# Issue order in the pooling stage of a two-layer decoder trunk: sums, transposes and the next layer's units

## The chip, the cores and the metric

The kernel runs on one core of a Trainium2 chip. The metric is the device time of one execution in microseconds (us), as the median of several runs; a profiled execution of the kernel before stands beside it. TensorE is called PE here (its weight loads PEld), VectorE DVE, ScalarE ACT, GpSimd POOL, SyncE SP. Each engine works through its own queue in the order in which the program issues its instructions, and semaphores hold an instruction until what it needs is there.

## The reference

The input is one sequence of 256 tokens with 2048 channels in float32. Two layers follow each other; each adds a mixer and then an MLP with squared ReLU (2048 to 8192 to 2048) to the residual x, each behind an RMS norm. Layer 0's mixer is a convolution beside sparse attention. Layer 1's mixer, where the change lies, takes four groups of 512 channels and, for a group g with the trailing window w of 2, 4, 8 or 16 tokens, forms

```python
parts.append((csg - shifted) / cnt[None, :, None] - xn[..., sl])   # mean of the last w tokens minus the token
y = jnp.einsum('bsgp,gpo->bsgo', p, pool_w).reshape(B, S, D_MODEL)   # per-group linear map
x = x + y * pool_scale
x = x + mlp(x, mlp_norm[1], w_mlp_in[1], w_mlp_out[1])
```

## The kernel before, in words

**Numbers.** A float32 product is made of three passes: each operand is split into a rounded high part and the rest, and high x high, high x low and low x high are added in PSUM. For weights, ACT writes the high part `whi` and DVE the rest `wlo`, each in two halves of 128x1024. For activations it is the same: `xT` holds both parts of a group of x, transposed.

**Weights.** All weights come as units of 128x2048 (1 MB), in the order of use. `W.next()`, called at the start of a unit, asks SP for the load of the unit four further on and issues the split (two ACT, two DVE instructions) of the unit two further on, ahead of the unit's own matmuls. Three buffers each hold raw, high and low units, so a split also waits for the unit before the current one to be done on PE, and a load for an earlier split.

**The stage.** It stands between the end of layer 0's MLP and the first units of layer 1's MLP. x is a tile of 2 token halves x 2048 channels. For each group g of 512 channels:

- `pool_project(g)` (L1239): one weight unit, 24 matmuls of 512 columns, `xT[g]` against the group's map, into two banks (one for each half of the tokens). `by_token` (L257) calls `between(k)` after each quarter of it.
- `pool_split(g)` (L1245): scales by the norm's factor r1 and splits the result into a high and a low part, two ACT and two DVE instructions of 128x512.
- `pool_mean(g)` (L1254): the token sums as six matmuls of 512 columns with constant matrices `pm`, and for each half of the tokens two DVE instructions: `pt` (times count and scale) and the addition to x.
- `turn_x(g, V_MLP1)` (L242): eight transposes of x's group into two banks, and then for each of the four rows of 128 channels an ACT instruction (high part) and a DVE instruction (rest). Where ACT and DVE read the same bank, they take turns.

`first_hidden` (L1032) is the start of layer 1's MLP: four units u, each of 48 matmuls of 256 columns, unit u on `xT[u]`, into four banks that stay open through all four; ft counts the four quarters of a unit, and behind the second quarter it calls a function from the list `turns`, if it was given one. `turn_x(3, V_MIX1)`, the last transposes for layer 1's mixer, is what `later` holds (L1283). `factor(ssq1)` (L1006) makes r1: two small DVE instructions on the sums of squares that ACT left, and a power on POOL.

**Order.** The program's order is written out by hand, and no planner moves anything. Banks come from a pool of eight, and the bank that was given back first is taken first. The order around the change is

```python
proj0; later (turn_x(3, V_MIX1)); proj1; r1; split0; proj2; mean0; split1; proj3
mean1; split2; turn0; unit 0; mean2; split3; turn1; unit 1; mean3; turn2; unit 2; turn3; unit 3
```

where turn0 to turn3 are `turn_x(g, V_MLP1)`.

Of the kernel before, what the change touches and what calls it, by code (L numbers as in the profile page):

```python
# [61 lines left out]
V_MIX0, V_MIX1, V_MLP0, V_MLP1, V_CB, V_LNG, V_LNB, V_PK, V_PV, V_PS, V_GF = 0, 16, 32, 48, 64, 72, 80, 88, 104, 120, 136  # L62
# [20 lines left out]
class Weights:  # L83
# [86 lines left out]
    def next(self, k=4):  # L170
        u = self.used
        self.used += 1
        self.load_to(u + AHEAD_SPLIT + AHEAD_DMA)
        self.advance(u + AHEAD_SPLIT + self.lead)
        parts = (self.raw.pop(u),) if u < PLAIN else self.parts.pop(u)
        return [t.rearrange("p (k f) -> p k f", k=k) for t in parts]
# [3 lines left out]
def trunk(ctx: ExitStack, tc: tile.TileContext, a: dict, out: bass.AP, dump: dict | None = None):  # L180
# [10 lines left out]
    def mm(out, w, x, **kw):  # L191
        n = int(np.prod(x.shape[1:]))
        pe[0] += max(4 * n / 2400, 0.214) if x.dtype == F32 else max(n / 2400 + 0.0025, 0.107)
        nc.tensor.matmul(out, w, x, **kw)  # L194
# [34 lines left out]
    def transpose(out, src):  # L229
        n = src.shape[0]  # L230
        pe[0] += 0.218
        nc.tensor.transpose(out, src, ident[0:n, 0:n])  # L232
# [5 lines left out]
    xT = [None] * 4  # L238
# [3 lines left out]
    def turn_x(dc, g0, bank):  # L242

        xT[dc] = act.tile([P, 4, 512], F32R, tag="xT", bufs=4, name="xT")
        for h in range(2):
            t = bank().rearrange("p (f t) -> p f t", f=2)
            for f in range(2):
                d = (4 * dc + 2 * h + f) * P
                for tok in range(2):
                    transpose(t[:, f, tok * P:(tok + 1) * P], x[:, tok, d:d + P])  # L250
            for f in range(2):
                dt = 4 * dc + 2 * h + f
                o, g = xT[dc][:, 2 * h + f], vec[:, g0 + dt:g0 + dt + 1]
                nc.scalar.activation(o[:, 0:256], t[:, f], AF.Copy, scale=g)
                vector.scalar_tensor_tensor(o[:, 256:512], t[:, f], g, o[:, 0:256].bitcast(F32),
                                            op0=ALU.mult, op1=ALU.subtract)

    def by_token(acc, X, hi, lo, first, last, between=None, outer=False):


        order = [(k, tok) for k in range(4) for tok in range(2)]
        if outer:
            order.sort(key=lambda o: o[1])
        for n, (k, tok) in enumerate(order):
            xh, xl = (X[:, k, i * 256 + tok * P:i * 256 + (tok + 1) * P] for i in range(2))
            mm(acc[tok], xh, hi[:, k], start=(first and k == 0), stop=False)
            mm(acc[tok], xh, lo[:, k], start=False, stop=False)
            mm(acc[tok], xl, hi[:, k], start=False, stop=(last and k == 3))
            if between is not None and n % 2:
                between(n // 2)  # L270


    with ExitStack() as mx:
# [4 lines left out]
        def acc1(n=256, dt=F32):  # L278
            return ps.tile([P, 512], dt, tag="acc", bufs=8, name="acc")[:, 0:n]
# [181 lines left out]
        for pr in range(2):  # L461
            for i in range(2):
                acc = acc1()
# [138 lines left out]
        def bank(tag, dt=F32):  # L602
            return ps.tile([P, 512], dt, tag=tag, bufs=2, name=tag)
# [255 lines left out]
        for j in range(8):  # L859
# [5 lines left out]
            acc = ab[j][:, 0:256]  # L865
# [95 lines left out]
        def bank3():  # L961
            return ps.tile([P, 512], F32, tag="acc", bufs=8, name="acc")
# [27 lines left out]
    def ssq_tile():  # L990
        return mlp.tile([P, 2, 4], F32, tag="ssq", bufs=2, name="ssq")
# [7 lines left out]
    def token_ms(ssq):  # L999

        ms = const.tile([P, 2], F32, tag="ms", bufs=2, name="ms")
        vector.tensor_reduce(ms, ssq, axis=AX, op=ALU.add)
        vector.tensor_scalar(ms, ms, 1.0 / D, EPS, op0=ALU.mult, op1=ALU.add)
        return ms

    def factor(ssq):  # L1006

        r = const.tile([P, 2], F32, tag="r", bufs=2, name="r")
        nc.gpsimd.tensor_tensor(r, token_ms(ssq), neg_half, op=ALU.pow)
        return r  # L1010

    def form(tag):
        return mlp.tile([P, 1024], F32R, tag=tag, bufs=1, name=tag)

    def hidden(acc, out):

        nc.scalar.activation(out, acc, AF.Relu)  # L1017
        nc.scalar.activation(out, out, AF.Square)  # L1018
# [10 lines left out]
    def t_tile():  # L1029
        return mlp.tile([P, 4, 256], F32, tag="t", bufs=3, name="t")  # L1030

    def first_hidden(turns=()):  # L1032

        accs = [bank3()[:, 0:256] for _ in range(4)]
        T[0, 0] = t_tile()
        for u in range(4):
            hi, lo = W.next()
            for ft in range(4):
                f = slice(ft * P, (ft + 1) * P)
                for k in range(4):  # L1040
                    Xh, Xl = (xT[u][:, k, i * 256:(i + 1) * 256] for i in range(2))
                    mm(accs[ft], hi[:, k, f], Xh, start=(u == 0 and k == 0), stop=False)
                    mm(accs[ft], hi[:, k, f], Xl, start=False, stop=False)
                    mm(accs[ft], lo[:, k, f], Xh, start=False, stop=(u == 3 and k == 3))
                if u == 3:
                    hidden(accs[ft], T[0, 0][:, ft])
                elif ft == 1 and turns:
                    turns.pop(0)()
            yield
# [170 lines left out]
    ssq1 = ssq_tile()  # L1220
# [15 lines left out]

    def pool_project(gi):  # L1239
        hi, lo = W.next()  # L1240
        acc = [bank3() for _ in range(2)]
        by_token(acc, xT[gi], hi, lo, True, True)
        return acc

    def pool_split(gi, acc):  # L1245
        z = [form(("s2", "s3", "s4", "f22")[2 * (gi % 2) + tok]).rearrange("p (i f) -> p i f", i=2) for tok in range(2)]
        for tok in range(2):
            nc.scalar.activation(z[tok][:, 0], acc[tok], AF.Copy, scale=r1[:, tok:tok + 1])
        for tok in range(2):
            vector.scalar_tensor_tensor(z[tok][:, 1], acc[tok], r1[:, tok:tok + 1], z[tok][:, 0].bitcast(F32),  # L1250
                                        op0=ALU.mult, op1=ALU.subtract)
        return z

    def pool_mean(gi, z):  # L1254
        for to in range(2):
            acc = bank3()
            terms = [(tok, i) for tok in range(to + 1) for i in range(2)]
            for n, (tok, i) in enumerate(terms):
                mm(acc, pm[:, tok + to, gi], z[tok][:, i], start=(n == 0), stop=(n == len(terms) - 1))
            c = slice(gi * 512, (gi + 1) * 512)  # L1260
            t = mlp.tile([P, 512], F32, tag="s", bufs=3, name="pt")
            vector.scalar_tensor_tensor(t, acc, count[:, to, gi:gi + 1], ps_row[gi], op0=ALU.mult, op1=ALU.mult)
            vector.tensor_add(x[:, to, c], x[:, to, c], t)

    def pool_and_first():

        pool_mean(1, z1)
        units = first_hidden()
        z2 = pool_split(2, proj2)
        turn_x(0, V_MLP1, bank3)  # L1270
        next(units)
        pool_mean(2, z2)
        z3 = pool_split(3, proj3)
        turn_x(1, V_MLP1, bank3)
        next(units)
        pool_mean(3, z3)
        turn_x(2, V_MLP1, bank3)
        next(units)
        turn_x(3, V_MLP1, bank3)
        yield from units  # L1280

    proj0 = pool_project(0)
    for f in later:  # L1283
        f()
    proj1 = pool_project(1)
    r1 = factor(ssq1)
    z0 = pool_split(0, proj0)
    proj2 = pool_project(2)
    pool_mean(0, z0)
    z1 = pool_split(1, proj1)  # L1290
    proj3 = pool_project(3)
    ssq2 = ssq_tile()
    gf_row = []

    def last(dc):
# [6 lines left out]
        return []  # L1302

    run_mlp(last, pool_and_first)
    rs = factor(ssq2)
    for h in range(2):
# [118 lines left out]
```

## Time and profile before

| | |
|---|---|
| median of 3 runs | 1805.62 us (1805.35 to 1809.41) |
| profiled execution | 1807.23 us, its span 1805.4 us |
| mean granted TensorE clock | 0.995 of 2.4 GHz |
| busy: PE, PEld, DVE, ACT, POOL | 1774.8, 1602.4, 1517.9, 1088.3, 57.9 us |
| weights and inputs read | 395.93 MB, 220 GB/s over the span |

Times in the trace count from the start of the span. A line of a timeline gives the start, the length, the engine, the line of the kernel, the operation, output <- input with their shapes, how many equal instructions were merged (x), and in brackets how long the engine had been idle before it and what ended that. Several matmuls overlap in the array, so a PE instruction's length is longer than its distance to the next start. Many instructions carry the line of a helper: L194 every matmul, L232 every transpose, L78 every DVE instruction, L147 the weights' high part, L254 the high part of `xT`.

### The profile page before, as it was taken

Reading aid. Unit: us, or ns where it says so; the run is one execution under the profiler, and the core shown is the slowest. Engines: PE = TensorE matmul, PEld = TensorE weight load, DVE = VectorE, ACT = ScalarE, POOL = GpSimd, SP = SyncE. Lnnn points to the kernel's source line nnn. Section 1 sums busy time; section 2 is a strip of 40 time slices with the busy share of each in tenths; the row PEclk is TensorE's granted clock in tenths of the full one; section 3 lists DMA queues with packets and bytes.
Section 4 is the critical chain, followed back from the end, with each engine's and each line's share of the span. In section 5 each row is a group of like instructions: output and inputs, shape, how many; then the busy total and the mean of one; then the engine's idle time right before and its main releaser. Section 6 shows DMA issues by size and latency. Waiting matters only on the chain.

```text
span 1805.4 us, 28697 instructions
## 1 busy us (share of the span) xinstructions
PE 1774.8 (98%) x11726; PEld 1602.4 (89%) x11726; DVE 1517.9 (84%) x1884; ACT 1088.3 (60%) x1626; POOL 57.9 (3%) x78
## 2 busy tenths in 40 slices
PE   9999999999999999999999998999999999999997
PEld 7999988889899899989898887989989998989885
DVE  6998886766889898898989767688989889898984
ACT  4445665547566666666666564766666656566653
POOL 1000000000000000000000000000000000000000
PEclk9999999999999999999999999999999999999998
DMA  7654222546778787878787753577878787877772
GB/s 278 237 184 151 105 94 90 214 169 218 245 247 268 237 250 233 284 237 273 233 259 244 244 203 117 189 244 247 275 239 254 234 270 236 286 233 250 246 242 102
DMA packets 58052, 399.89 MB, mean 221 GB/s; under 512 B 6560, under 2 KB 6960, under 8 KB 10816
## 3 DMA queue, kind: packets, MB, share of 16 engines
q1 hardware_dynamic: 47760, 333.47, 48.3%
q0 software_dynamic: 8576, 61.43, 18.2%
q10 hardware_dynamic: 1584, 3.16, 0.5%
q8 instruction: 92, 1.51, 0.3%
q14 instruction: 40, 0.33, 0.0%
HBM read 395.93 MB, written 2.10 MB: 220 GB/s over the span
## 4 chain that ended last, share of the span: by engine, by line
PE 76%; DVE 20%; ACT 2%; issue 1%; DMA 1%; ACTq 0%; POOLq 0%; SPq 0%; DVEq 0%
PE acc L194 71%; DVE wlo L78 9%; DVE z L78 3%; DVE s L78 3%; PE S L194 2%; DVE x L78 2%; PE PV L194 1%; ACT whi L147 1%; PE T L232 1%; DVE f L78 1%; DMA xraw<-in_xT 0%; PE acc L232 0%; ACT t L1018 0%; DVE pt L78 0%; ACT t L1017 0%
## 5 line engine op out<-in xcount | busy, mean ns | idle before, releaser
L194 PE MATMUL acc<-xT,whi 128*128 128x256 f32 x4992 | 880.5, 280 | 6.5 <-DVE xT L78 5.2
L194 PEld LDWEIGHTS acc<-xT,whi 128*128 128x128 f32 x4992 | 768.3, 189 | 20.5 <-DVE xT L78 8.3
L78 DVE TENSOR_TENSOR wlo<-wraw,whi 128x1024 fp32r<-128x1024 f32 (+1 forms) x552 | 604.9, 1126 | 148.3 <-ACT whi L147 147.0
L194 PE MATMUL acc<-xT,wlo 128*128 128x256 f32 x2496 | 695.3, 279 | 0.0
L147 ACT ACTIVATE whi<-wraw 128x1024 fp32r<-128x1024 f32 (+1 forms) x552 | 514.5, 973 | 91.4 <-PE acc L194 65.9
L194 PEld LDWEIGHTS acc<-xT,wlo 128*128 128x128 f32 x2496 | 472.4, 189 | 0.0
L194 PE MATMUL acc<-whi,s 128*128 128x512 f32 x960 | 318.3, 393 | 2.8 <-DVE s L78 1.6
L78 DVE TENSOR_TENSOR wlo<-z,whi 128x1024 fp32r<-128x1024 f32 x224 | 266.9, 1218 | 48.3 <-ACT whi L147 47.3
L147 ACT ACTIVATE whi<-z 128x1024 fp32r<-128x1024 f32 x224 | 230.6, 1054 | 93.9 <-DVE z L78 67.9
L194 PE MATMUL acc<-whi,f 128*128 128x512 f32 x864 | 282.9, 392 | 0.0
L194 PEld LDWEIGHTS acc<-whi,s 128*128 128x128 f32 x960 | 179.2, 188 | 42.6 <-DVE s L78 7.5
L1017 ACT ACTIVATE t<-acc 128x256 f32<-128x256 f32 x128 | 48.9, 382 | 252.9 <-PE acc L194 252.2
L194 PE MATMUL acc<-wlo,s 128*128 128x512 f32 x480 | 190.6, 397 | 1.1
L194 PEld LDWEIGHTS acc<-whi,f 128*128 128x128 f32 x864 | 162.3, 188 | 32.5
L194 PE MATMUL acc<-wlo,f 128*128 128x512 f32 x432 | 169.4, 392 | 0.0
L78 DVE SCALAR_TENSOR_TENSOR x<-acc,r,x 128x512 f32<-128x512 f32 x156 | 115.9, 745 | 13.5 <-PE acc L194 13.5
L194 PEld LDWEIGHTS acc<-wlo,s 128*128 128x128 f32 x480 | 90.1, 188 | 27.6 <-DVE wlo L78 9.1
L78 DVE SCALAR_TENSOR_TENSOR ctile<-ctile,cw 128x256 f32<-128x256 f32 x240 | 102.0, 481 | 0.0
L194 PEld LDWEIGHTS acc<-wlo,f 128*128 128x128 f32 x432 | 81.1, 188 | 15.9
L1062 ACT ACTIVATE s<-s 128x512 fp32r<-128x512 f32 x56 | 35.4, 632 | 71.9 <-DVE s L78 71.9
L78 DVE TENSOR_TENSOR z<-z,b 128x1024 f32<-128x1024 f32 x56 | 65.9, 1219 | 0.0
L78 DVE TENSOR_TENSOR z<-z,wraw 128x1024 f32<-128x1024 f32 x56 | 65.9, 1218 | 0.0
(205 smaller groups left out, 1366.4 us busy)
## 6 DMA issues: line engine op xcount, KB each, us to landing
wraw<-in_ws SPq DMA_DIRECT2D x254, 1024.0 KB, 5.9
z<-in_ws SPq DMA_DIRECT2D x28, 1024.0 KB, 7.4
b<-in_ws SPq DMA_DIRECT2D x28, 1024.0 KB, 4.8
b<-in_ws POOLq DMA_DIRECT2D x28, 1024.0 KB, 8.8
z<-in_ws POOLq DMA_DIRECT2D x28, 1024.0 KB, 8.0
xraw<-in_xT SPq DMA_DIRECT2D x4, 512.0 KB, 7.3
wraw<-in_ws SPq DMA_DIRECT2D x8, 256.0 KB, 7.6
w<-in_cmp_w POOLq DMA_DIRECT2D x2, 1024.0 KB, 7.4
```

Of the source, the lines that this page charges most:

```text
L78: return fn(*args, **kw)
L147: nc.scalar.activation(hi[:, c], raw[:, c], AF.Copy)
L194: nc.tensor.matmul(out, w, x, **kw)
L232: nc.tensor.transpose(out, src, ident[0:n, 0:n])
L1017: nc.scalar.activation(out, acc, AF.Relu)
L1062: nc.scalar.activation(F[tag][:, :, 0:P], src(), AF.Copy)
```

## The change

The instructions stay the same; their order in the program is another, and with it that of each engine's queue. `factor(ssq1)` is issued before `later`. `pool_mean(0)` and `turn_x(0, V_MLP1)` are issued in the middle of projections 2 and 3. The splits 2 and 3 stand around `pool_mean(1)`, ahead of unit 0. The transposes of groups 1 to 3 are issued in the middle of units 0 to 2, by the list that `first_hidden` takes.

```diff
-    def pool_project(gi):
+    def pool_project(gi, midway=lambda: None):
         hi, lo = W.next()
         acc = [bank3() for _ in range(2)]
-        by_token(acc, xT[gi], hi, lo, True, True)
+        by_token(acc, xT[gi], hi, lo, True, True, lambda k: midway() if k == 1 else None)
         return acc
...
     def pool_and_first():
-        pool_mean(1, z1)
-        units = first_hidden()
-        z2 = pool_split(2, proj2)
-        turn_x(0, V_MLP1, bank3)
+        units = first_hidden([lambda dc=dc: turn_x(dc, V_MLP1, bank3) for dc in (1, 2, 3)])
         next(units)
         pool_mean(2, z2)
-        z3 = pool_split(3, proj3)
-        turn_x(1, V_MLP1, bank3)
         next(units)
         pool_mean(3, z3)
-        turn_x(2, V_MLP1, bank3)
-        next(units)
-        turn_x(3, V_MLP1, bank3)
         yield from units

     proj0 = pool_project(0)
+    r1 = factor(ssq1)
     for f in later:
         f()
     proj1 = pool_project(1)
-    r1 = factor(ssq1)
     z0 = pool_split(0, proj0)
-    proj2 = pool_project(2)
-    pool_mean(0, z0)
+    proj2 = pool_project(2, lambda: pool_mean(0, z0))
     z1 = pool_split(1, proj1)
-    proj3 = pool_project(3)
+    proj3 = pool_project(3, lambda: turn_x(0, V_MLP1, bank3))
+    z2 = pool_split(2, proj2)
+    pool_mean(1, z1)
+    z3 = pool_split(3, proj3)
     ssq2 = ssq_tile()
```

## Rows read from the trace of the kernel before

**Rows 1.** The page's first lines: the span, and each engine's busy time with its share of the span and its instructions.

```profile
span 1805.4 us, 28697 instructions
PE 1774.8 (98%) x11726; PEld 1602.4 (89%) x11726; DVE 1517.9 (84%) x1884; ACT 1088.3 (60%) x1626; POOL 57.9 (3%) x78
```

**Rows 2.** Busy time of each engine in three stretches: projections 1 to 3 with two sums, the four units of `first_hidden` with what stands between them, and a stretch of the MLP behind it. The columns are the length, the busy time (and instructions) of PE, PEld, DVE, ACT and POOL, the granted clock, the DMA engines' mean busy share, and GB/s.

```profile
1076.75:1097.90 21.15, 21.15 (x101) 17.39 (x99) 17.80 (x25) 11.87 (x18) 0.71 (x1) 1.00 0.44 152
1097.90:1141.30 43.40, 36.13 (x229) 31.00 (x229) 26.03 (x38) 17.72 (x32) 0.00 (x0) 0.92 0.40 147
1186.50:1245.90 59.40, 59.40 (x399) 54.75 (x400) 50.25 (x50) 36.19 (x47) 1.73 (x2) 1.00 0.78 259
```

**Rows 3.** Who waited for whom between 1060 and 1150 us: the sum, how many times, and the longest.

```profile
DVE pt L78 <- PE acc L194: 6.6, 2, 3.4
...
PE acc L194 <- DVE xT L78: 5.2, 3, 2.5
```

**Rows 4.** PE's timeline, the first lines of what follows each other in the stage.

```profile
1076.75 1.03 PE L232 MATMUL acc<-ident,x 128*128 128x128 f32 x8
1077.54 0.48 PE L194 MATMUL acc<-whi,xT 128*128 128x512 f32 x1
...
1088.62 1.56 PE L194 MATMUL acc<-s,pm 128*128 128x512 f32 x6
1090.03 0.39 PE L194 MATMUL acc<-whi,xT 128*128 128x512 f32 x1
...
1095.52 1.10 PE L194 MATMUL acc<-s,pm 128*128 128x512 f32 x4
...
1096.92 1.04 PE L232 MATMUL acc<-ident,x 128*128 128x128 f32 x8
1098.08 0.38 PE L194 MATMUL acc<-xT,whi 128*128 128x256 f32 x1
1100.95 0.39 PE L194 MATMUL acc<-xT,whi 128*128 128x256 f32 x1 [2.48 <-DVE xT L78]
...
1108.73 1.56 PE L194 MATMUL acc<-s,pm 128*128 128x512 f32 x6
...
1111.60 0.66 PE L232 MATMUL acc<-ident,x 128*128 128x128 f32 x4 [0.73 <-DVE pt L78]
...
1114.04 0.38 PE L194 MATMUL acc<-xT,whi 128*128 128x256 f32 x1 [1.66 <-DVE xT L78]
...
1125.95 0.38 PE L194 MATMUL acc<-xT,whi 128*128 128x256 f32 x1 [1.03 <-DVE xT L78]
...
1137.97 0.39 PE L194 MATMUL acc<-xT,whi 128*128 128x256 f32 x2
...
1138.31 0.39 PE L194 MATMUL acc<-xT,whi 128*128 128x256 f32 x2
```

**Rows 5.** The columns of rows 2, in stretches of two microseconds.

```profile
1102.00:1104.00 2.00, 2.00 (x9) 1.94 (x10) 1.00 (x3) 1.65 (x3) 0.00 (x0) 0.50 0.00 0
...
1116.00:1118.00 2.00, 2.00 (x10) 1.77 (x10) 1.54 (x2) 1.80 (x2) 0.00 (x0) 0.50 0.00 0
...
1120.00:1122.00 2.00, 2.00 (x20) 2.00 (x19) 0.00 (x0) 0.00 (x0) 0.00 (x0) 1.00 0.94 246
...
1126.00:1128.00 2.00, 1.85 (x9) 1.25 (x9) 1.02 (x3) 1.42 (x4) 0.00 (x0) 1.00 0.00 0
```

**Rows 6.** DVE's timeline.

```profile
1078.59 0.48 DVE L78 SCALAR_TENSOR_TENSOR xT<-acc,vec,xT 128x256 fp32r<-128x256 f32 x1
...
1081.98 2.36 DVE L78 TENSOR_TENSOR wlo<-wraw,whi 128x1024 fp32r<-128x1024 f32 x2 [0.47 <-ACT whi L147]
1084.26 0.15 DVE L78 TENSOR_REDUCE ms<-ssq 128x2 f32<-128x8 f32 x1
1084.44 0.17 DVE L78 TENSOR_SCALAR ms<-ms 128x2 f32<-128x2 f32 x1
...
1087.69 2.36 DVE L78 TENSOR_TENSOR wlo<-wraw,whi 128x1024 fp32r<-128x1024 f32 x2
1089.96 0.74 DVE L78 SCALAR_TENSOR_TENSOR pt<-acc,count,t 128x512 f32<-128x512 f32 x1
...
1092.74 0.74 DVE L78 SCALAR_TENSOR_TENSOR s<-acc,r,s 128x512 fp32r<-128x512 f32 x1
...
1094.06 2.35 DVE L78 TENSOR_TENSOR wlo<-wraw,whi 128x1024 fp32r<-128x1024 f32 x2
...
1113.51 0.47 DVE L78 SCALAR_TENSOR_TENSOR xT<-acc,vec,xT 128x256 fp32r<-128x256 f32 x1
...
1115.94 0.48 DVE L78 SCALAR_TENSOR_TENSOR xT<-acc,vec,xT 128x256 fp32r<-128x256 f32 x1 [0.54 <-ACT xT L254]
1116.89 2.36 DVE L78 TENSOR_TENSOR wlo<-wraw,whi 128x1024 fp32r<-128x1024 f32 x2 [0.46 <-ACT whi L147]
```

**Rows 7.** ACT's and POOL's timeline (L1017 is the ReLU behind the last quarter of unit 3).

```profile
1080.89 2.00 ACT L147 ACTIVATE whi<-wraw 128x1024 fp32r<-128x1024 f32 x2
1085.44 1.27 ACT L1248 ACTIVATE s<-acc,r 128x512 fp32r<-128x512 f32 x2 [2.56 <-POOL r L1009]
...
1141.57 0.38 ACT L1017 ACTIVATE t<-acc 128x256 f32<-128x256 f32 x1 [0.53 <-PE acc L194]
...
1084.70 0.71 POOL L1009 TENSOR_TENSOR r<-ms,neg_half 128x2 f32<-128x2 f32 x1 [82.18 <-DVE ms L78]
```

## The prediction

> **What bounds the kernel now.** I read the page's first lines first: PE is busy for 1774.8 of 1805.4 us [rows 1], so time can only come from stretches in which PE is not at its pace. The table by stretches finds the one the change touches: behind it, in the MLP, PE is busy for 59.40 of 59.40 us, and in the projections for 21.15 of 21.15, but in the four units of the next layer only for 36.13 of 43.40 [rows 2]. The waits name the cause: PE waits for DVE's part of `xT` (5.2 us in three waits), and DVE in turn waits twice, 6.6 us together, for PE's sums [rows 3]. The timeline shows how these belong together. After each sum come the transposes and then at once the unit that reads them: the unit issues one matmul and stands still for 2.48, 1.66 and 1.03 us [rows 4], because DVE first has the sum's `pt` and x, then a split, and only then `xT`. Once the unit runs, DVE has nothing left until the next sum. Two engines work by turns.
>
> **How much is there.** By the busy column the stretch holds 43.40 - 36.13 = 7.3 us to be had [rows 2]. I don't use that column: PE reads 2.00 of 2.00 both with 9 or 10 matmuls and with 20 [rows 5]. The Trainium skill warns of it too ("Trainium Kernel Development and Optimization", Performance Expectations): matmul busy time tells badly how close a kernel is to its limit, since matmuls are pipelined. By the busy column the time could not fall below 1798.3; by the count that follows it can fall by twice that.
>
> The count, which I use: three matmuls of 256 columns go from 1137.97 to 1138.31, 0.1137 us each [rows 4], a unit of 48 is 5.46 and half a unit 2.73. A sum of six is 1090.03 - 1088.62 = 1.41, eight transposes 1077.54 - 1076.75, about 0.8; a projection of 24 is 1095.52 - 1090.03 = 5.49 [rows 4]. Unit 3's last matmuls start by 1141.3 (ACT takes up their result at 1141.57) [rows 7]. From 1097.9 to there are four units, two sums and three turns: 21.84 + 2.82 + 2.4 = 27.1 of 43.4 us. So 16.3 us at most can go. Part of it is the clock: granted at 0.50 from 1102 to 1104 and from 1116 to 1118 [rows 5], behind the waits of 2.48 and 1.66 us [rows 4].
>
> **The change, part by part.** Nothing is added or removed; queues are reordered. DVE's prices, from one start to the next: a split of a weight unit 1089.96 - 1087.69 = 2.27; a sum's four instructions 1092.74 - 1089.96 = 2.78; a `pool_split` 1094.06 - 1092.74 = 1.32; a turn 2.9 (1113.51 to 1115.94 + 0.48), waits for ACT of 0.54 in it included [rows 6].
>
> *factor earlier.* Its two small instructions (0.15 + 0.17) [rows 6] now stand ahead of the last turn for the mixer, which starts at 1078.9 instead of 1078.59, and the split at 1081.98 moves to 1082.3. POOL's 0.71 [rows 7] then ends near 1079.7; nothing else was waiting on POOL's queue, which had been idle for 82 us. In return ACT no longer waits for r1 (2.56) [rows 7]: its weight split (from 1080.89) ends some 1.9 later plus the shift, near 1083.1, and split 0 follows. On DVE: weight split to 1084.6, split 0 to 1085.9. If r1 came late after all, the middle of projection 2 would show it; the cover is 3.4 us (1079.7 to 1083.1).
>
> *mean0 in projection 2.* Projection 1 starts near 1077.6, the middle of projection 2 is 1.5 x 5.49 later, at 1085.9, just as split 0 ends; its last term is read 1.1 us after that. I cost it at nothing; bounds 0 to 1.3 (split 0 late by its own length).
>
> *turn0 in projection 3.* DVE: weight split to 1088.2, mean0's x to 1091.0, split 1 to 1092.3, weight split to 1094.6, turn0 to 1097.5. PE: projection 3's middle at 1092.8 (1085.9 + 1.41 + 2.73 + 2.73), x ready 1.8 us before. Projection and sum 1 end at 1097.8 and unit 0 finds `xT` complete, where it stood 2.48 us before and then ran on behind DVE and at half clock. The start of unit 0 is the old one, within 0.3 us.
>
> *Units 0 to 3.* DVE goes on: split 2 (0.1 for ACT) to 1098.9, mean1 to 1101.7, split 3 to 1103.0, weight split to 1105.2, turn1 to 1108.2, mean2 to 1110.9, weight split to 1113.1, turn2 to 1116.0, mean3 to 1118.8, weight split to 1121.0, turn3 to 1123.9. PE against it:
>
> - Unit 0 from 1097.8; its half at 1100.55 waits for x of group 1 until 1101.7, 1.1 us. Everything behind the transposes on PE's queue waits too; the other half unit is what is queued there. Turn and half to 1105.3, sum 2 to 1106.7.
> - Unit 1 needs its last row of `xT` at its eleventh matmul, 1107.8, and has it at 1108.2: 0.4. Half at 1109.8, x at 1110.9: 1.1. Turn, half, sum 3 to 1115.9.
> - Unit 2: `xT` at 1116.0 is in time; half at 1118.6, x at 1118.8: 0.2. To 1122.4.
> - Unit 3: last row at 1123.5 wanted, 1123.9 had: 0.4. End 1122.4 + 5.46 + 0.4 = 1128.3.
>
> So of 16.3 us of loss some 3.2 stay, and unit 3 ends 1141.3 - 1128.3 = 13.0 us earlier. What is late next is DVE: from 1082 to 1124 its queue hardly rests, and PE is at most 1.1 us ahead of it. The waits are nearest to the one of 1.03, behind which the clock stayed at 1.00 through 1126 to 1128 [rows 4, 5], so I take no fall.
>
> *What could take it back.* Banks: given out in the order of their return, unit 0's four are turn0's and projection 2's (read out by 1097.5 and 1098.9, the latter first wanted at 1100.5), later turns get those of the turn before. The old order paid 0.73 here (turn1 got sum 2's banks [rows 4]); the new one nothing, at most that. Weight loads move with the DVE splits that free their buffers; SP passes nothing new and only follows its order. The stretch asks for 147 GB/s over 43.4 us, 210 over 30.4, and the MLP is served at 259 with PE never idle [rows 2]. ACT's weight splits, which wait for PE to leave a buffer, have the length of a sum on DVE in hand. Bounds here: 0 to 2 us.
>
> **The sum.** The profiled execution took 1807.23 us, 1.83 around its span, which the change leaves alone: 1807.23 - 13.0 = 1794.2. It stands 1.6 above the median of the runs, so the median becomes 1805.62 - 13.0 = 1792.6.
>
> **The rivals.**
>
> *The clock falls again* (0.15). Two waits of 1.1 us now stand inside units, and halves of a unit are cut by transposes. The Trainium skill ("Perfetto Trace Analysis", Matmul Optimizations) speaks against that: the engine scales its power with use, so matmuls should run in unbroken batches; the trace shows such falls, behind 2.48 and 1.66, not behind 1.03 us. At half clock 9 matmuls start in 2.00 us, 0.22 each [rows 5] instead of 0.114; a fall that holds for the two microseconds of a row, or for as long again, costs 9 to 18 times 0.1, some 1.5 us, and two cost 3: 1794 to 1796.
>
> *DVE is slower than my walk* (0.12). The walk has the turn's own 0.54 waits once, and none of the 0.46 that DVE spends behind a turn on ACT [rows 6]. With 1.0 more for each of five turns, all on the path, unit 3 ends 5 us later: 1797.6.
>
> *It doesn't do what it says, or is lost behind* (0.08): r1 or x comes as late as before, or the MLP behind is paced by its loads and not by PE. 1805 to 1806. Against it: PE's 59.40 of 59.40 [rows 2].
>
> *Slower* (0.04). One mechanism: the clock stays at half from the first wait, 1101.7, to the end of unit 3, since each further wait comes before it has risen. 168 matmuls of 256 columns at 0.1 more and 12 of 512 at 0.2 more cost 19 us, DVE's lag of 2 hides in it, and 17 - 13 = +4: 1809.6; with the first unit behind it at half too, 48 x 0.1 = 4.8 more: 1814.4. It decides if a second wait falls inside the half-clock stretch; the rows had the clock back at 1.00 by 1120 with the same spacing of waits.
>
> *Forecast* (0.61): losses of 0 to 5 us instead of 3.2, 1789.3 to 1794.3.
>
> **The numbers.** 0.3% (5.4 us) is about what a measurement of this kernel can tell from no change. Forecast, clock and slow DVE are faster: 0.88, of which 0.01 may end inside the 5.4. The third rival is the same, and the fourth lies for three quarters beyond the bound: 0.87 faster, 0.08 + 0.01 + 0.01 = 0.10 the same, 0.03 slower. The range reaches from PE's floor (1805.62 - 16.3 = 1789.3) to beyond the second rival's 1797.6, at 1798.8, so that hardly more than the last two rivals' 0.12 is left out, and some of the second.
>
> **What would show it.** Right: the matmul sums of group 0 between two halves of projection 2 without a wait ahead of them; ACT's split 0 with no wait for POOL; unit 0's first matmuls unbroken; PE's waits named x (`pt`), one of about a microsecond in each of units 0 and 1; granted clock 1.00 throughout; unit 3's end near 1128. Wrong: a wait for a bank or a weight half in the stage, a clock of 0.50, DVE idle for long between 1085 and 1124, or PE at less than its pace in the first chunk of the MLP, where the 13 us would then have gone.

## The result, and the profile after

The changed kernel takes 1792.28 us in the median (1787.79 to 1795.08, 4 runs) against 1805.48 us for the kernel before, measured beside it: ratio 0.9912, 95% interval 0.9892 to 0.9933. That is 13.2 us less; 1792.6 was forecast. Its profiled execution took 1794.04 us with a span of 1792.3.

The whole time of this kernel spreads by 3 to 4 us to either side, and most of that comes from outside the stage: in two profiled executions of it the stage differed by 0.1 us and the way to it by 3.2. So most of what follows is told by one distance inside it, the *stage*: from the first transpose of the mixer's last turn on PE to ACT's ReLU behind the last quarter of unit 3. Before it is 1141.57 - 1076.75 = 64.82 us [rows 4, 7], after 1129.65 - 1078.33 = 51.32: 13.5 us less.

```profile
1078.33 1.03 PE L232 MATMUL acc<-ident,x 128*128 128x128 f32 x8
...
1129.65 0.38 ACT L1017 ACTIVATE t<-acc 128x256 f32<-128x256 f32 x1 [0.53 <-PE acc L194]
```

In the profiled executions the changed kernel comes to the stage 1.6 us later and gains 1.2 us behind it, neither of which the change touches.

The stretches that answer to [rows 2], with the same columns (length; busy time of PE, PEld, DVE, ACT, POOL with instructions; granted clock; DMA share; GB/s): the projections, the four units, and a stretch of the MLP.

```profile
1078.33:1099.40 21.07, 21.07 (x101) 17.50 (x100) 18.24 (x28) 13.05 (x21) 0.71 (x1) 1.00 0.56 193
1099.40:1129.40 30.00, 28.65 (x229) 27.20 (x228) 24.45 (x35) 16.19 (x28) 0.00 (x0) 1.00 0.42 155
1174.60:1234.00 59.40, 59.40 (x404) 54.68 (x405) 50.36 (x51) 37.44 (x48) 1.72 (x2) 1.00 0.78 259
```

The same 229 matmuls and transposes that took 43.4 us now take 30.0, at full clock, with nearly the same DVE and ACT work (24.45 and 16.19 us, where [rows 2] have 26.03 and 17.72) beside them. The MLP behind runs as before. Who waits for whom between 1060 and 1150 us, for [rows 3]:

```profile
ACT xT L254 <- DVE xT L78: 12.0, 12, 2.9
...
PEld acc L232 <- DVE x L78: 1.5, 2, 1.0
PE acc L232 <- DVE x L78: 1.1, 2, 0.8
PEld acc L194 <- DVE xT L78: 0.7, 2, 0.3
```

PE's matmuls (L194) no longer wait for `xT`, which was 5.2 us; only their weight loads do, for 0.7. What is new is a wait of the transposes (L232) for x. PE's timeline shows the two:

```profile
1087.46 1.56 PE L194 MATMUL acc<-s,pm 128*128 128x512 f32 x6
1088.87 0.39 PE L194 MATMUL acc<-whi,xT 128*128 128x512 f32 x1
...
1094.36 1.03 PE L232 MATMUL acc<-ident,x 128*128 128x128 f32 x8
1095.15 0.48 PE L194 MATMUL acc<-whi,xT 128*128 128x512 f32 x1
...
1098.94 0.63 PE L194 MATMUL acc<-f,pm 128*128 128x512 f32 x2
1099.40 0.40 PE L194 MATMUL acc<-xT,whi 128*128 128x256 f32 x2
...
1102.23 0.27 PE L232 MATMUL acc<-ident,x 128*128 128x128 f32 x1
1102.81 0.98 PE L232 MATMUL acc<-ident,x 128*128 128x128 f32 x7 [0.30 <-DVE x L78]
...
1110.95 0.27 PE L232 MATMUL acc<-ident,x 128*128 128x128 f32 x1
1112.01 0.98 PE L232 MATMUL acc<-ident,x 128*128 128x128 f32 x7 [0.79 <-DVE x L78]
...
1119.80 1.09 PE L232 MATMUL acc<-ident,x 128*128 128x128 f32 x8
```

The sum of group 0 (1087.46) and its transposes (1094.36) stand inside projections without a wait. Unit 0 begins at 1099.40 with no gap, where [rows 4] had 2.48 us. In each of units 0 and 1 the first of eight transposes, which reads the first half of the tokens, runs, and the second is held until DVE has added the second half. From first to last matmul, without turns (and the waits in them) and sums, unit 0 takes 5.7 us instead of 10.7, unit 1 6.1 instead of 10.0, unit 2 5.7 instead of 8.3.

### The profile page after: what moved, and what is told of

The parts are those of the page before. It is cut to its first block, busy times and chain, and to the rows that moved or that the text cites. A ratio compares the mean times of both kernels' runs of the same rounds, so it can differ in the third digit from the quotient of the medians.

```text
span 1792.3 us, 28698 instructions
## 1 busy us (share of the span) xinstructions
PE 1767.5 (99%) x11726; PEld 1599.5 (89%) x11726; DVE 1517.0 (85%) x1884; ACT 1088.4 (61%) x1626; POOL 57.8 (3%) x78
## 4 chain that ended last, share of the span: by engine, by line
PE 72%; DVE 22%; ACT 3%; issue 2%; DMA 1%; ACTq 0%; POOLq 0%; SPq 0%; DVEq 0%
PE acc L194 68%; DVE wlo L78 11%; DVE z L78 3%; DVE s L78 3%; PE S L194 2%; DVE x L78 2%; ACT whi L147 1%; PE PV L194 1%; PE T L232 1%; DVE xT L78 1%; DVE f L78 1%; DMA xraw<-in_xT 0%; ACT xT L254 0%; ACT t L1018 0%; ACT sq L997 0%
## 5 line engine op out<-in xcount | busy, mean ns | idle before, releaser
L194 PE MATMUL acc<-xT,whi 128*128 128x256 f32 x4992 | 874.1, 279 | 0.3
L194 PEld LDWEIGHTS acc<-xT,whi 128*128 128x128 f32 x4992 | 765.8, 188 | 10.5 <-DVE xT L78 0.7
L194 PE MATMUL acc<-xT,wlo 128*128 128x256 f32 x2496 | 694.9, 278 | 0.0
L194 PEld LDWEIGHTS acc<-xT,wlo 128*128 128x128 f32 x2496 | 470.8, 189 | 0.0
L194 PE MATMUL acc<-whi,s 128*128 128x512 f32 x960 | 318.6, 393 | 2.7 <-DVE s L78 1.6
L194 PE MATMUL acc<-whi,f 128*128 128x512 f32 x864 | 283.1, 392 | 0.0
L194 PEld LDWEIGHTS acc<-whi,s 128*128 128x128 f32 x960 | 179.5, 188 | 42.0 <-DVE s L78 7.4
L1017 ACT ACTIVATE t<-acc 128x256 f32<-128x256 f32 x128 | 48.8, 382 | 252.9 <-PE acc L194 252.4
L194 PE MATMUL acc<-wlo,s 128*128 128x512 f32 x480 | 190.8, 398 | 1.2
L194 PEld LDWEIGHTS acc<-whi,f 128*128 128x128 f32 x864 | 162.5, 188 | 32.1
L194 PE MATMUL acc<-wlo,f 128*128 128x512 f32 x432 | 169.5, 392 | 0.0
L78 DVE SCALAR_TENSOR_TENSOR x<-acc,r,x 128x512 f32<-128x512 f32 x156 | 115.5, 742 | 13.5 <-PE acc L194 13.5
L194 PEld LDWEIGHTS acc<-wlo,s 128*128 128x128 f32 x480 | 90.2, 188 | 28.1 <-DVE wlo L78 9.7
L194 PEld LDWEIGHTS acc<-wlo,f 128*128 128x128 f32 x432 | 81.2, 188 | 16.0
```

The costliest lines, as they stand in the source:

```text
L78: return fn(*args, **kw)
```

## The experiments

Each kernel is one edit, and the one called both together is two. Single runs don't rank by their whole time: the way to the stage alone differed by 5 us between two profiled executions of one kernel, and by 13 over all. The last to come there, at 1085.28, is the one with three more DVE instructions, and the edit is not why: in that execution the clock was granted at 0.51 from 288 to 312 us, long before the edit. So the stage is compared. Beside it stands DVE's lead into the stage: by how much its weight split for projection 2 starts ahead of the transposes that mark the stage's beginning. It was not looked at before the runs. Before and changed:

```profile
1076.31 2.36 DVE L78 TENSOR_TENSOR wlo<-wraw,whi 128x1024 fp32r<-128x1024 f32 x2 [2.42 <-ACT whi L147]
...
1077.40 2.36 DVE L78 TENSOR_TENSOR wlo<-wraw,whi 128x1024 fp32r<-128x1024 f32 x2 [2.42 <-ACT whi L147]
```

| kernel | stage, us | against the changed one | DVE's lead, us |
|---|---|---|---|
| before | 64.82 | +13.5 | 0.44 |
| changed; again on another occasion | 51.32; 51.46 | 0; +0.1 | 0.93; 0.79 |
| r1 late | 53.62 | +2.3 | 0.48 |
| transposes behind the units | 59.21 | +7.9 | 0.73 |
| before, with the transposes in the units alone | 55.99 | +4.7 | 0.86 |
| three more DVE instructions | 53.64 | +2.3 | 0.42 |
| before, PE kept at work | 62.74 | +11.4 | 0.89 |
| crosswise evacuation; again | 48.76; 48.76 | -2.6 | 2.22; 2.22 |
| splits one unit later | 50.47 | -0.9 | 0.46 |
| crosswise and later splits | 48.76 | -2.6 | 2.23 |

**r1 late.** Of the change, the early `factor` alone is undone.

```diff
-    r1 = factor(ssq1)
     for f in later:
         f()
     proj1 = pool_project(1)
+    r1 = factor(ssq1)
```

> The stage is measured from the first transpose of the mixer's last turn on PE to ACT's ReLU behind unit 3: 64.82 us before (1076.75 to 1141.57), 51.32 changed (1078.33 to 1129.65). This kernel is the changed one with factor(ssq1) back behind projection 1. Theory (DVE's queue is the bound of the new order from split 0 on): r1 comes behind one more weight split, split 0 ends some 1.9 us later, PE waits about 0.8 us in the middle of projection 2 for the sum of group 0, and DVE carries the 1.9 us through to unit 3: stage 53.0 to 53.4. Rival (the place of r1 does not matter, PE's own order is the bound): stage 51.3, within 0.4.

Measured: 53.62. PE's lines show the chain: a wait in the middle of projection 2, and then longer ones for x.

```profile
1083.62 1.44 PE L194 MATMUL acc<-s,pm 128*128 128x512 f32 x5 [0.29 <-DVE s L78]
...
1098.85 0.33 PE L232 MATMUL acc<-ident,x 128*128 128x128 f32 x1 [0.41 <-DVE x L78]
1100.23 0.98 PE L232 MATMUL acc<-ident,x 128*128 128x128 f32 x7 [1.06 <-DVE x L78]
```

ACT's first `pool_split` again waited 2.55 us for POOL. The move of two instructions of 0.3 us is worth some 1.9 us, as expected (of the 2.3 measured, 0.45 go with the smaller lead), since what they hold up stands at the head of DVE's queue.

**Transposes behind the units.** The changed kernel, with the half-unit shift of turns 1 to 3 undone.

```diff
-        units = first_hidden([lambda dc=dc: turn_x(dc, V_MLP1, bank3) for dc in (1, 2, 3)])
+        units = first_hidden()
         next(units)
         pool_mean(2, z2)
+        turn_x(1, V_MLP1, bank3)
         next(units)
         pool_mean(3, z3)
+        turn_x(2, V_MLP1, bank3)
+        next(units)
+        turn_x(3, V_MLP1, bank3)
         yield from units
```

> The changed kernel with the transposes of groups 1 to 3 back between the units (behind the sum of the group after), all else as changed. Theory: units 1, 2 and 3 again wait for DVE's sum and then xT; the waits of about 2.5 us come back ahead of units 1 and 2 and one of about 1 us ahead of unit 3, and with them perhaps a half-clock stretch: stage 58 to 61, so that the half-unit shift of the transposes is worth 7 to 10 of the 13.5 us. Rival (the early r1, splits and sums carry the gain): stage 51 to 54.

Measured: 59.21. The old pattern is back, one matmul and then a wait. The waits are shorter than expected, 1.76 us ahead of unit 1 and 1.03 ahead of unit 2; the rest of the loss is PE running behind DVE's rows of `xT`, and the clock. Behind the first wait the clock (the column before the DMA share) is down in the two microseconds from 1112:

```profile
1106.80 0.38 PE L194 MATMUL acc<-xT,whi 128*128 128x256 f32 x1
1108.94 0.38 PE L194 MATMUL acc<-xT,whi 128*128 128x256 f32 x1 [1.76 <-DVE xT L78]
...
1119.68 0.38 PE L194 MATMUL acc<-xT,whi 128*128 128x256 f32 x1
1121.10 0.38 PE L194 MATMUL acc<-xT,whi 128*128 128x256 f32 x1 [1.03 <-DVE xT L78]
...
1112.00:1114.00 2.00, 2.00 (x11) 2.00 (x11) 2.00 (x2) 0.70 (x1) 0.00 (x0) 0.53 0.03 8
```

**Transposes in the units, alone.** The kernel before with that part only.

```diff
-        units = first_hidden()
+        units = first_hidden([lambda dc=dc: turn_x(dc, V_MLP1, bank3) for dc in (1, 2, 3)])
...
-        turn_x(1, V_MLP1, bank3)
         next(units)
         pool_mean(3, z3)
-        turn_x(2, V_MLP1, bank3)
-        next(units)
-        turn_x(3, V_MLP1, bank3)
         yield from units
```

> The kernel before with one part of the change alone: the transposes of groups 1 to 3 in the middle of units 0 to 2. Theory: unit 0 keeps its loss of some 5 us (2.5 us of waiting, running behind DVE, half clock), the later units lose as little as in the changed kernel: stage 55 to 56.5. Rival (the shift only pays with the splits ahead of unit 0, since split 3 now stands between the sum of group 2 and xT): stage above 60.

Measured: 55.99. Unit 0 keeps its wait, and the units behind it have lost theirs but for 0.35 us in the middle of unit 2:

```profile
1098.44 0.38 PE L194 MATMUL acc<-xT,whi 128*128 128x256 f32 x1
1101.17 0.39 PE L194 MATMUL acc<-xT,whi 128*128 128x256 f32 x1 [2.35 <-DVE xT L78]
...
1122.71 0.27 PE L232 MATMUL acc<-ident,x 128*128 128x128 f32 x1
1123.33 0.98 PE L232 MATMUL acc<-ident,x 128*128 128x128 f32 x7 [0.35 <-DVE x L78]
```

The two parts nearly add up. This part alone gives 64.82 - 55.99 = 8.8 us, and the rest of the change alone (the kernel of the experiment ahead of this one) 64.82 - 59.21 = 5.6; together that is 0.9 more than the 13.5 of both at once.

**Three more DVE instructions.** The suspected bound, made longer: products that nobody reads, behind split 1.

```diff
+    for _ in range(3):
+        t = mlp.tile([P, 512], F32, tag="s", bufs=3, name="extra")
+        vector.tensor_mul(t, ps_row[0], ps_row[1])
     proj3 = pool_project(3, lambda: turn_x(0, V_MLP1, bank3))
```

> The changed kernel with three more DVE instructions of 128x512 (about 0.7 us each, 2.1 together, their result read by nobody) behind split 1. Theory (DVE is the bound from there to unit 3): the time goes through to the end: stage 53.0 to 53.5, seen as longer waits for x in unit 0. Rival (PE is the bound and DVE has slack): stage 51.3 to 51.8.

Measured: 53.64 (1085.28 to 1138.92), 2.3 more than the changed kernel. DVE's timeline gives the three 1.8 us, and the lead is 0.5 smaller here: both went through to the end. The wait for x in the middle of unit 0 is where the time shows: it was one of 0.30 us and is now two, of 1.02 and 1.06. The later waits are no longer than they were.

```profile
1110.70 0.33 PE L232 MATMUL acc<-ident,x 128*128 128x128 f32 x1 [1.02 <-DVE x L78]
1112.09 0.98 PE L232 MATMUL acc<-ident,x 128*128 128x128 f32 x7 [1.06 <-DVE x L78]
```

**Crosswise evacuation.** The suspected bound, made shorter. In a turn of the changed kernel DVE waits twice for ACT, whose high part of the row it subtracts. ACT in its turn starts the second row of a bank only when DVE is done with the first:

```profile
1106.26 0.47 DVE L78 SCALAR_TENSOR_TENSOR xT<-acc,vec,xT 128x256 fp32r<-128x256 f32 x1
1107.28 0.88 DVE L78 SCALAR_TENSOR_TENSOR xT<-acc,vec,xT 128x256 fp32r<-128x256 f32 x2 [0.54 <-ACT xT L254]
1108.70 0.48 DVE L78 SCALAR_TENSOR_TENSOR xT<-acc,vec,xT 128x256 fp32r<-128x256 f32 x1 [0.55 <-ACT xT L254]
1109.10 0.74 DVE L78 SCALAR_TENSOR_TENSOR pt<-acc,count,t 128x512 f32<-128x512 f32 x1
...
1108.19 0.48 ACT L254 ACTIVATE xT<-acc,vec 128x256 fp32r<-128x256 f32 x1 [0.58 <-DVE xT L78]
```

With both banks transposed first, each engine finds the other bank free.

```diff
+        t = []
         for h in range(2):
-            t = bank().rearrange("p (f t) -> p f t", f=2)
+            t.append(bank().rearrange("p (f t) -> p f t", f=2))
             for f in range(2):
...
+        for f in range(2):
+            part = [(xT[dc][:, 2 * h + f], vec[:, g0 + 4 * dc + 2 * h + f:g0 + 4 * dc + 2 * h + f + 1], t[h][:, f])
+                    for h in range(2)]
+            for o, g, s in part:
+                nc.scalar.activation(o[:, 0:256], s, AF.Copy, scale=g)
+            for o, g, s in part:
+                vector.scalar_tensor_tensor(o[:, 256:512], s, g, o[:, 0:256].bitcast(F32),
+                                            op0=ALU.mult, op1=ALU.subtract)
```

> The changed kernel with another order inside turn_x: both banks are transposed first, then ACT and DVE go through them crosswise (first row of either bank, then second row of either), so that DVE no longer waits 0.54 us twice for ACT in a turn. All five turns of the stage and those of layer 0 have it. Theory (DVE is the bound): DVE's part of a turn goes from 2.9 to 1.8 us, some 1.1 less per turn; PE's remaining waits of 2.2 us go down to under 0.7: stage 49.0 to 49.7, the whole some 2 us under the changed kernel. Rival (PE's own order is the bound): stage 51.3, within 0.3.

Measured: 48.76, less than expected. DVE's turn, from its first instruction to the next group's `pt`, takes 1106.87 - 1105.06 = 1.8 us instead of 1109.10 - 1106.26 = 2.8; PE is busy throughout the four units (last line: 1099.20 to 1126.70, columns as above), and at one place DVE now waits for PE (0.40):

```profile
1105.06 0.87 DVE L78 SCALAR_TENSOR_TENSOR xT<-acc,vec,xT 128x256 fp32r<-128x256 f32 x2
1106.08 0.88 DVE L78 SCALAR_TENSOR_TENSOR xT<-acc,vec,xT 128x256 fp32r<-128x256 f32 x2 [0.15 <-ACT xT L256]
1106.87 0.74 DVE L78 SCALAR_TENSOR_TENSOR pt<-acc,count,t 128x512 f32<-128x512 f32 x1
...
1114.21 0.75 DVE L78 SCALAR_TENSOR_TENSOR pt<-acc,count,t 128x512 f32<-128x512 f32 x1 [0.40 <-PE acc L194]
...
1099.20:1126.70 27.50, 27.50 (x229) 26.90 (x228) 23.26 (x34) 16.52 (x28) 0.00 (x0) 1.00 0.43 164
```

No wait of PE is left in the stage. So DVE was the bound, and PE is now. The Trainium skill ("PSUM — Partial Sum Buffer", PSUM bank collisions raise a hardware error) has two engines kept off one bank at the same time, reads by ACT and DVE included; ACT's wait for DVE of 0.58 us between two rows of a bank is in accord with such a guard, and the edit keeps the guard and takes away most of the waiting. The lead of 2.22 us says that part of this comes from the turns ahead of the stage, which have the new order too. The whole: median 1792.03 us in 6 runs, ratio 0.989 (0.9858 to 0.9922), beside runs of the kernel before that spread from 1803.6 to 1824.0.

**Splits one unit later.** Another way to unload DVE.

```diff
+        W.lead = 0
         next(units)
         pool_mean(2, z2)
         next(units)
         pool_mean(3, z3)
+        next(units)
+        W.lead = 1
         yield from units
```

> The changed kernel with the weight splits issued one unit ahead instead of two through units 0 to 2, and two splits in unit 3. Theory: DVE has one weight split (2.27 us) less ahead of each of turn1, turn2 and turn3, so the waits for x and xT shrink: stage 49.2 to 49.8, if the late splits are still in time for their units. Rival (PE is the bound): 51.3; rival (a weight half comes late): PE waits for wlo at the start of unit 2, 3 or the one behind it, stage or what follows longer by about 1 us.

Measured: 50.47; 49.2 to 49.8 was expected, and neither rival fits. Part of it is the marker: two splits stand ahead of the ReLUs on ACT's queue in unit 3. By the next unit's ReLU the gain is 56.76 - 55.62 = 1.1 us. The waits in units 1 to 3 are gone, but the one in unit 0 is not, and is even longer (0.8 us in the table of waits, where the changed kernel has 1.1 for both of its own): x of group 1 stands ahead of the splits that were moved, and the lead was 0.46 us. The expectation overlooked the first and knew nothing of the second. The whole: 1792.38 us, ratio 0.9898 (0.9868 to 0.9928).

**Both together.**

> The changed kernel with the crosswise evacuation and the later splits together. Theory: DVE no longer limits, PE runs at its pace: 0.8 + 3 x 5.49 + 2 x 1.41 + 0.8 + 4 x 5.46 + 2 x 1.41 + 3 x 0.8 + 0.3 for the ReLU = 48.2 us is the floor; stage 48.2 to 49.0, the whole 2.5 to 3 us under the changed kernel. Rival: a new wait for a weight half takes its place, stage 49.5 or more.

Measured: 48.76, the same as the crosswise evacuation alone; with PE at its pace there was nothing left for the later splits. The whole: 1789.0 us, ratio 0.9876 (0.9844 to 0.9908).

**Before, with PE kept at work.** 24 and 18 matmuls on constants fill the two long waits of the kernel before.

```diff
             hi, lo = W.next()
+            if len(turns) == 0 and u < 2 and fill:
+                spare = bank3()[:, 0:256]
+                for _ in range(fill[u]):
+                    mm(spare, pm[:, 0, 0], pm[:, 1, 0:2].rearrange("p g t -> p (g t)"), start=True, stop=True)
...
-        units = first_hidden()
+        units = first_hidden(fill=(24, 18))
```

> The kernel before with PE kept at work in its two long waits: 24 matmuls of 256 columns on constants ahead of unit 0 and 18 ahead of unit 1, into a bank that nobody reads. This tells what the two half-clock stretches were worth. Theory (most of the gain is waiting, the clock only adds to it): the granted clock stays at 1.00 and the stage falls by 1 to 2.5 us, to 62.3 to 63.8. Rival (the clock is most of it): stage 60 or less.

Measured: 62.74, 2.1 less than before. The filling starts in the waits, and the clock is 1.00 over the whole stretch:

```profile
1095.60 3.12 PE L194 MATMUL acc<-pm 128*128 128x256 f32 x24
...
1109.84 2.42 PE L194 MATMUL acc<-pm 128*128 128x256 f32 x18 [0.73 <-DVE s L78]
...
1094.00:1140.00 46.00, 42.26 (x308) 37.22 (x307) 28.37 (x41) 20.67 (x37) 0.00 (x0) 1.00 0.42 160
```

Counted from the stage's beginning, sum 2 starts 1.0 us earlier than before and sum 3 2.1, so each of the two stretches gives about half. The conditions are not quite equal: the second filling lasts until 1112.10, some 1.3 us longer than the wait for the first row of `xT` would have (DVE has written it by 1110.83), though the unit behind it then runs without a stop, and DVE's lead is 0.45 larger. So the two half-clock stretches were worth about 2 of the 13.5 us; the other 11 or so are PE waiting for DVE or running behind it.

**The changed kernel and the crosswise one, side by side.**

> The changed kernel again, beside the next one on one chip. Stage 51.3 within 0.3 in the profile; the whole 10 to 17 us under the kernel before, with a spread of some 3 us either way that comes from outside the stage.

> The crosswise evacuation again. Theory (DVE was the bound, and is no longer): stage 48.8 within 0.3, and the median 1 to 4 us under that of the changed kernel beside it. Rival (the 2.6 us are lost behind the stage): the same median within 0.5 us.

Measured: stages 51.46 and 48.76. The whole, against 1805.05 us before: 1792.79 us for the changed kernel (1790.42 to 1796.42; ratio 0.9926, 0.9905 to 0.9946), 1786.88 for the crosswise one (1782.58 to 1787.50; ratio 0.9886, 0.9863 to 0.9909). The crosswise kernel's six runs all lie below the six of the changed one; from both together it can't be told apart (ratios 0.9886 and 0.9876, with overlapping intervals). The difference of the medians, 5.9 us, is more than the 2.6 of the stage and more than was expected; in the earlier runs, on another chip, its median was 5 us higher. What the evacuation gives outside the stage (it also serves layer 0) was not taken apart.

## Why the prediction was right

**The step that carried it holds:** two engines worked by turns, and the new order lets them work side by side. The gain forecast was 13.0 us, the stage gave 13.5 and the whole 13.2. That the medians, 1792.6 forecast and 1792.28 measured, agree to 0.3 us is luck: the runs spread over 7 us.

**What bounds, and the floor.** The floor by count was 16.3 us below the old time; the crosswise kernel is 64.82 - 48.76 = 16.1 below it in the stage, with no wait left. The busy column, which would have allowed 7.3, was the wrong measure, as the prediction said: PE's busy time in the four units went from 36.13 to 28.65 us for the same matmuls. On this the trace agrees with the Trainium skill's warning cited there. Of the two measures that the Trainium skill proposes instead ("Perfetto Trace Analysis", Identifying the Most-Contended Engine), the share of the peak work was not worked out here, and the busy share of the weight loads falls short too: PEld reads 31.00 of 43.40 before [rows 2] and 27.20 of 30.00 after for the same loads, so that column by itself would have allowed 12.4 us.

**factor earlier.** Costed at 0.3 us of DVE with a cover of 3.4: right, ACT's split 0 came without a wait for POOL, whose r1 ended 3.3 us ahead of it:

```profile
1080.12 0.71 POOL L1009 TENSOR_TENSOR r<-ms,neg_half 128x2 f32<-128x2 f32 x1 [76.02 <-DVE ms L78]
...
1084.14 1.25 ACT L1248 ACTIVATE s<-acc,r 128x512 fp32r<-128x512 f32 x2
```

What a late split 0 would cost was bounded at 1.3 us; undoing the move cost some 1.9, so that bound was too small: it counted the split's length, but neither the weight split ahead of r1 nor POOL.

**mean0 and turn0 in projections 2 and 3.** Costed at nothing, and no wait stands ahead of either.

**Units 0 to 3.** Waits were forecast at 1.1, 0.4 and 1.1, 0.2, 0.4 us. Start to start, less the 0.11 of a matmul, PE lost about 0.5 in unit 0, 0.3 and 0.95 in unit 1, nothing in unit 2 and 0.3 in unit 3: 2.05 instead of 3.2. The places are right but for unit 2, the size in unit 0 is half: the walk began with the lead of the trace of before, 0.44 us, and DVE had 0.93. About half a microsecond was lost again by pace (below); 0.341 us for three matmuls was assumed throughout. Lead and pace, neither of them foreseen, partly cancel.

**"What is late next is DVE"**: shown from both sides. More work or later work on DVE goes through to the end (+2.3 and +2.3, lead included), less of it takes PE's waits away (-2.6).

**The rivals.** The clock stayed at 1.00 in the stage of the changed kernel, so the first did not come about. The second, DVE slower by 1.0 per turn, did not come about: DVE ended its last turn 46.6 us into the stage, where the walk had 47.15, and the half microsecond is what its lead was larger. So the walk's prices were right. The third falls because the whole lost as much as the stage. The prediction's own argument against it, PE's 59.40 of 59.40 us in the MLP, rests on the busy column that it had set aside; the count behind it is what tells, 399 instructions in 59.40 us before and 404 after, both at a clock of 1.00. The fourth falls with the clock.

## What to carry to other kernels

When two engines hand the same groups to and fro, half a unit of other work between the hand-overs can be worth more than any of the instructions: nothing was made shorter here, and 13 us went. Then walk the queue of the engine that is not the bottleneck, from one start to the next: it became the bound, and 1.1 us of its own waiting in each turn was the next thing to remove. Where the whole time spreads by more than the edit gives, measure the stage between two instructions that every version has.

## What the runs showed of the hardware that was not expected

**The matmul stream has more than one pace at full clock.** In the changed kernel three matmuls of 256 columns take 0.353 us at the start of unit 0 (1099.76 to 1100.82, nine) and 0.340 behind the wait in its middle (1103.99 to 1105.01), both at a granted clock of 1.00:

```profile
1099.76 0.40 PE L194 MATMUL acc<-xT,whi 128*128 128x256 f32 x2
...
1100.82 0.40 PE L194 MATMUL acc<-xT,whi 128*128 128x256 f32 x2
...
1103.99 0.39 PE L194 MATMUL acc<-xT,whi 128*128 128x256 f32 x2
...
1105.01 0.39 PE L194 MATMUL acc<-xT,whi 128*128 128x256 f32 x2
```

It keeps one pace over many matmuls and often has another behind a gap. A unit of 48 differs by 0.2 us, which adds up in the MLPs and is a part of the spread between executions: between 470 and 1030 us, in layer 0's MLP, the two traces of the changed kernel have 814 and 512 matmuls that start 0.117 to 0.119 us behind the one before. By an estimate, 302 times 0.004 us are 1.2 of the 3.2 us by which the first comes later to the stage. What sets the pace stays open.

**Two waits of a microsecond in a row did not bring the clock down.** The granted clock fell to 0.50 behind waits of 2.48 and 1.66 us (before) [rows 5] and 2.35 us (transposes in the units, alone; 0.50 from 1104 to 1106), and to 0.53 over two microseconds behind 1.76 (transposes behind the units). It stayed at 1.00 behind 1.03 us. It also stayed at 1.00, from 1110 to 1114, where waits of 1.02 and 1.06 us stood with one transpose between them (three more DVE instructions), though together they are longer than the 1.66. No run here tells what decides.
